# A hybrid decoder block on one core: GpSimd's low parts among mixing's last products wait for norm 2's last scaled half

## The chip, the cores and the metric

The kernel runs on one core of one Trainium2 chip. The time is the device time of one execution in microseconds. It was run three times before the change: 783.74, 784.01 and 784.80 us, median 784.01 us.

## The reference

One block of a decoder over 512 tokens of width 1024, all in float32:

```
h = rmsnorm(x, norm1_g);  z = h @ w_in + b_in          # 1024 -> 6656, five parts
u = glu(z);  u = conv31(u);  y_a = silu(layernorm(u)) @ conv_w_out + conv_b_out
xb = conv4(z_rx);  hb = rg_lru(xb);  y_b = (hb * gelu(z_rg)) @ lru_w_out
m = sigmoid(z_ga) * y_a + sigmoid(z_gb) * y_b
x = x + m @ w_mix_out
h = rmsnorm(x, norm2_g)
x = x + (silu(h @ ffn_w1) * (h @ ffn_w3)) @ ffn_w2      # 1024 -> 2816 -> 1024
out = rmsnorm(x, norm_f_g)
```

`rmsnorm(x, g)` is x / sqrt(mean(x * x) + 1e-6) * g over a row. What the change concerns lies between `x + m @ w_mix_out` and the first products of `h @ ffn_w1`.

## The kernel before

Every matrix product is made of three. A weight comes from HBM as a raw tile of 128x1024 in float32; ScalarE casts it to float32r (the high part, line 129), and VectorE or GpSimd subtracts the high part from the raw tile (the low part, line 125). TensorE then adds high by high, high by low and low by high. A chunk of weights is cast and split some chunks before it is used: `weights(key, ahead)` emits the chunks up to `ahead` behind the one that is asked for, so the casts and low parts of FFN weights are issued among mixing's last products. Which engine makes a low part is set where the chunk is listed. Of the first FFN chunks, `fb11_1`, `fb21_1` and `fb11_2` have GpSimd (`pool_e`), and `fb21_2` has VectorE. The buffers `hl_...` hold the two parts, `raw_...` the raw tile; eight raw tiles are in turn, and SyncE loads a new one once the low part made from the old one is done.

The larger products use seven products of half size in place of eight (Strassen's scheme), so their results are combined on VectorE from banks of PSUM. In `mix_end` (line 1478), mixing's last part, this is the order that is written out by hand for TensorE, ScalarE and VectorE:

- `second()`: the last products but those of the quarter `t4`; VectorE adds and subtracts the banks into `x2`, the residual stream in rows (four tiles of 128 tokens, `x2[t]`, in two halves of 512 columns each).
- For the first rows, t = 0 and 1: the root of the mean square (ScalarE, lines 686, 693 and 694; VectorE, lines 679 and 696), and then `scale` (line 1484): VectorE multiplies each half by it into `xs[t][half]`. Halves 0 of both rows come first, then halves 1; the last of the four is `xs11`. `newest["scaled"]` names the newest of these instructions.
- `newest["behind"]` is set to that last one while `third(i, range(2))` issues the products of `t4` for k = 0 and 1, and reset to None behind them. `third` asks for weights, so the cast and the low part of FFN chunks are emitted in this stretch.
- Twice: `turn_half` and two more products of `t4`. `turn_half` has TensorE transpose eight blocks of `xs` (line 712, banks `th`, four chunks of 128 columns by two rows). ScalarE copies each chunk out, multiplied by the norm's weight, as the high part `h20h` to `h27h` (line 715), and VectorE makes the low part `h20l` to `h27l` from the bank and the high part (line 716). Each of the second four chunks takes over the bank of one of the first four: `th04` waits for `h20l`, `th05` for `h21l`, and so on.
- Then GpSimd adds `h2` back from its parts (`full`, line 1476), VectorE finishes the other two rows, and these are scaled too.

Behind `mix_end` the FFN's first products begin: `b0.half` multiplies `h20` to `h27` of the first rows with `fb11_1` and `fb21_1` (banks `fr`, line 1584), `b1.half` with `fb11_2` and `fb21_2`; the second half of the rows is turned among them.

GpSimd's own order is not written out by hand: it takes its instructions as the scheduler places them, each with the waits that its data need. `tc.issue_after(i)` (line 133) orders the instructions of its block behind `i` only on the engine of `i` itself. As `newest["behind"]` is an instruction of VectorE, the line orders low parts on VectorE and says nothing on those of GpSimd.

Of the kernel before, what the change touches and what calls it, by code (L numbers as in the profile page):

```python
# [8 lines left out]
F32 = mybir.dt.float32  # L9
# [78 lines left out]
def tile_block(ctx, tc, a, out):  # L88
# [30 lines left out]
    newest = {}  # L119
    put_off = []  # L120

    SYNC = mybir.DependencyInfo(mybir.DependencyClass.Sync, mybir.DependencyReason.DATA)

    def sub(eng, o, x, y):
        return eng.tensor_tensor(out=o, in0=x, in1=y, op=ALU.subtract)  # L125

    def split_to(h, l, full, eng, copy=act.copy):

        newest["cast"] = copy(h, full)  # L129
        if eng is None:  # L130
            put_off.append((l, full, h.bitcast(F32)))
            return h, l
        with tc.issue_after(newest["behind"]) if newest.get("behind") else nullcontext():
            last = sub(eng, l, full, h.bitcast(F32))
        newest["sub" if eng is pool_e else "low"] = last.ins
        return h, l

# [16 lines left out]
    def split(name, full, eng, p_=None, copy=act.copy):  # L154
        p_ = p_ or pairt(name)
        return split_to(*p_, full, eng, copy)
# [25 lines left out]
    def emit_chunk():  # L182
        key, src, kt, cols, where, lo, after = chunks[emitted[0]]
        if emitted[0] not in loaded_raw:
            load_chunk(emitted[0])
        raw = loaded_raw.pop(emitted[0])
        emitted[0] += 1
        n = kt * cols
        rv = raw[:, :n]
        if where == "gate":  # L190
            hl = hls.tile([P, 2, 1024], F32R, tag="hl", name=f"hl_{key}")
            h = hl[:, 0, :n]
            after(rv, h)
            held[key] = h
        elif where == "hl" or callable(where):
            hl = hls.tile([P, 2, 1024], F32R, tag="hl", name=f"hl_{key}")

            if emitted[0] == 1:
                h, l = first_parts(hl[:, 0, :n], hl[:, 1, :n], rv)
            else:  # L200
                h, l = split_to(hl[:, 0, :n], hl[:, 1, :n], rv, lo, act.copy if emitted[0] > 2 else copy_halves)
            held[key] = (h.rearrange("p (k n) -> p k n", k=kt), l.rearrange("p (k n) -> p k n", k=kt))
            if after:
                after()
        else:
            held[key] = [
                split_to(longt(f"{key}h{i}", F32R), longt(f"{key}l{i}", F32R), rv[:, i * T : (i + 1) * T], lo)
                for i in range(2)
            ]
# [1403 lines left out]
    class Seven:  # L1613
# [14 lines left out]
        def copy(self):  # L1628
            self.c11 = shortt(f"c11_{self.k}")
            left_over(act.copy(self.c11, self.r1).ins)  # L1630
# [248 lines left out]
```

## Time and profile before

| What | Time (us) |
|---|---|
| three runs | 783.74, 784.01, 784.80; median 784.01 |
| profiled execution | 783.79 |
| its span, from the first instruction to the last | 782.0 |
| mean granted TensorE clock | 0.999 |
| norm 2's first scaling (line 1484) begins | 438.8 |
| the first FFN products begin (line 1584) | 446.2 |
| output products begin (line 1331, banks `or`) | 671.4 |

In the views of the profile a row of a timeline gives the start and the duration in us from the span's start, the engine, the line, the operation, the tiles (written from read, buffer numbers left out), the shapes, the count where rows were merged, and in brackets the idle time ahead and what ended it. PE is TensorE's matmuls, PEld its loads of the stationary operand, DVE VectorE, ACT ScalarE, POOL GpSimd, SPq the queue of SyncE. In a row of waits stand who waited and for whom, the sum in us, how often, and the longest. A row of the chain has start, duration and what it was. A tile's row has the least, the median and the longest duration in ns, and the first and last start.

### The profile page before, as it was taken

Reading aid. Unit: us, or ns where it says so; the run is one execution under the profiler, and the core shown is the slowest. Engines: PE = TensorE matmul, PEld = TensorE weight load, DVE = VectorE, ACT = ScalarE, POOL = GpSimd, SP = SyncE. Lnnn points to the kernel's source line nnn. Section 1 sums busy time; section 2 is a strip of 40 time slices with the busy share of each in tenths; the row PEclk is TensorE's granted clock in tenths of the full one; section 3 lists DMA queues with packets and bytes.
Section 4 is the critical chain, followed back from the end, with each engine's and each line's share of the span. In section 5 each row is a group of like instructions: output and inputs, shape, how many; then the busy total and the mean of one; then the engine's idle time right before and its main releaser. Section 6 shows DMA issues by size and latency. Waiting matters only on the chain.

```text
span 782.0 us, 12628 instructions
## 1 busy us (share of the span) xinstructions
PE 774.8 (99%) x4469; PEld 684.1 (87%) x4469; DVE 677.2 (87%) x1034; ACT 490.4 (63%) x739; POOL 289.7 (37%) x239
## 2 busy tenths in 40 slices
PE   9999999999999999999999999999999999999997
PEld 8988888888888888888998898999999999888886
DVE  6389998889997987799999869779888889999957
ACT  8543678976786687567564676445555455666844
POOL 4365856577677973211100581312222220000001
PEclk9999999999999999999999999999999999999999
DMA  8827978696999995399986577998989794679522
GB/s 247 233 57 205 257 211 235 174 270 196 258 239 281 314 277 189 115 251 326 304 278 186 160 246 226 231 309 199 277 222 253 251 212 135 216 228 306 169 68 107
DMA packets 184752, 174.39 MB, mean 223 GB/s; under 512 B 14682, under 2 KB 145906, under 8 KB 184690
## 3 DMA queue, kind: packets, MB, share of 16 engines
q1 hardware_dynamic: 166034, 131.39, 57.1%
q0 software_dynamic: 18496, 41.95, 22.6%
q8 instruction: 35, 0.57, 0.3%
q14 instruction: 27, 0.22, 0.1%
q10 hardware_dynamic: 160, 0.27, 0.1%
HBM read 149.97 MB, written 50.33 MB: 256 GB/s over the span
## 4 chain that ended last, share of the span: by engine, by line
PE 97%; DVE 1%; DMA 1%; ACT 0%; issue 0%; SPq 0%; DVEq 0%
PE z L667 36%; PE fr L1584 25%; PE or L1331 13%; PE yb L667 7%; PE ya L1408 5%; PE mxr L1331 4%; PE f L667 3%; PE g L1155 2%; PE fr L1647 1%; DMA x<-in_x_dram 1%; DVE xs L1484 1%; PE tx L728 0%; PE th L712 0%; PE z L785 0%; DVE x L125 0%; DVE x L116 0%
## 5 line engine op out<-in xcount | busy, mean ns | idle before, releaser
L920 DVE SCALAR_TENSOR_TENSOR cv<-u,par,cv 128x507 f32<-128x507 f32 (+15 forms) x240 | 162.1, 732 | 4.2 <-ACT cv L916 3.4
L125 POOL TENSOR_TENSOR hl_in<-raw_in,hl_in 128x1024 fp32r<-128x1024 f32 (+1 forms) x52 | 124.7, 2417 | 66.6 <-ACT hl_in L129 61.6
L1584 PE MATMUL fr<-hs_0h,hl_ft 128*128 128x256 f32 x320 | 59.2, 283 | 0.0
L129 ACT CAST hl_in<-raw_in 128x1024 fp32r<-128x1024 f32 x50 | 51.5, 1048 | 1.1 <-DMA th<-tg 0.8
L1584 PEld LDWEIGHTS fr<-hs_0h,hl_ft 128*128 128x128 f32 x320 | 50.6, 192 | 0.0
L125 POOL TENSOR_TENSOR hl_ot<-raw_ot,hl_ot 128x1024 fp32r<-128x1024 f32 x1 | 2.4, 2411 | 121.3 <-ACT hl_ot L129 121.3
L508 POOL DMA_DIRECT2D ot<-in_ffn_w_dram x24 | 26.4, 1112 | 54.3 <-DVE hl_ft L125 33.3
L1584 PE MATMUL fr<-hs_0l,hl_ft 128*128 128x256 f32 x160 | 45.3, 283 | 0.0
L129 ACT CAST hl_fb<-raw_fb 128x1024 fp32r<-128x1024 f32 x30 | 31.3, 1047 | 21.5 <-PE fr L1584 10.9
L125 DVE TENSOR_TENSOR hl_fb<-raw_fb,hl_fb 128x1024 fp32r<-128x1024 f32 x27 | 33.3, 1234 | 10.4 <-ACT hl_fb L129 9.4
L667 PE MATMUL z<-h10h,hl_in 128*128 128x512 f32 (+1 forms) x108 | 41.1, 382 | 0.0
L667 PE MATMUL z<-h13h,hl_in 128*128 128x512 f32 (+1 forms) x108 | 40.8, 379 | 0.0
L667 PE MATMUL z<-h11h,hl_in 128*128 128x512 f32 (+1 forms) x108 | 40.8, 379 | 0.0
L667 PE MATMUL z<-h15h,hl_in 128*128 128x512 f32 (+1 forms) x108 | 40.8, 379 | 0.0
L667 PE MATMUL z<-h17h,hl_in 128*128 128x512 f32 (+1 forms) x108 | 40.8, 379 | 0.0
L667 PE MATMUL z<-h12h,hl_in 128*128 128x512 f32 (+1 forms) x108 | 40.8, 379 | 0.0
L667 PE MATMUL z<-h16h,hl_in 128*128 128x512 f32 (+1 forms) x108 | 40.8, 379 | 0.0
L667 PE MATMUL z<-h14h,hl_in 128*128 128x512 f32 (+1 forms) x108 | 40.8, 379 | 0.0
L129 ACT CAST hl_ft<-raw_fb 128x1024 fp32r<-128x1024 f32 x28 | 28.6, 1049 | 14.9 <-DVE raw_fb L116 11.8
L117 POOL TENSOR_TENSOR fws<-fws 128x256 f32<-128x256 f32 x44 | 36.5, 830 | 2.1
L129 ACT CAST hl_ob<-raw_ob 128x1024 fp32r<-128x1024 f32 (+1 forms) x23 | 23.4, 1015 | 21.1 <-PE or L1331 14.7
L125 DVE TENSOR_TENSOR hl_ft<-raw_fb,hl_ft 128x1024 fp32r<-128x1024 f32 x28 | 33.6, 1217 | 1.2 <-ACT hl_ft L129 1.2
(965 smaller groups left out, 2682.8 us busy)
## 6 DMA issues: line engine op xcount, KB each, us to landing
raw_in<-in_w_in_dram SPq DMA_DIRECT2D x51, 512.0 KB
raw_fb<-in_ffn_w_dram SPq DMA_DIRECT2D x74, 256.0 KB
ot<-in_ffn_w_dram POOLq DMA_DIRECT2D x30, 512.0 KB, 8.1
raw_ob<-in_ffn_w_dram SPq DMA_DIRECT2D x33, 256.0 KB
raw_ot<-ot SPq DMA_DIRECT2D x33, 256.0 KB
fws<-in_ffn_w_dram SPq DMA_DIRECT2D x12, 512.0 KB
cot<-in_conv_w_out_dram POOLq DMA_DIRECT2D x12, 512.0 KB, 8.6
mxt<-in_w_mix_out_dram POOLq DMA_DIRECT2D x12, 512.0 KB, 9.6
```

The costliest lines, as they stand in the source:

```text
L117: plus_on = lambda eng, o, x, y: eng.tensor_tensor(out=o, in0=x, in1=y, op=ALU.add)
L125: return eng.tensor_tensor(out=o, in0=x, in1=y, op=ALU.subtract)
L129: newest["cast"] = copy(h, full)
L508: plus = lambda o, x: pool_e.dma_start(o, x, accum_op=ALU.add)
L667: pe.matmul(ps, l, r, start=i == 0, stop=i == n - 1)
L920: vec.scalar_tensor_tensor(out=acc[:, s:], in0=u[c][:, : T - s], scalar=dw(c, s), in1=acc[:, s:], op0=ALU.mult, op1=ALU.add)
L1155: pe.matmul(ps[:HB], head_chunk[0][:ROWS_G, g, h % 2, m, :], ext[h][m][:ROWS_G], start=m == 0, stop=m == 1)
L1331: pe.matmul(banks[i][:, cs], l_[:, ts], r_[:, cs], start=start and n == 0, stop=stop and n == 2, skip_group_check=again)
L1408: pe.matmul(ps[:, HALVES[i]], lw[:, c, cols], rx_, start=not (again or i or c or m), stop=bool(i and c == 3 and m == 2), skip_group_check= ...
L1484: newest["scaled"] = vec.tensor_scalar(out=sc[t][i], in0=x2[t][i], scalar1=r, scalar2=None, op0=ALU.mult).ins
L1584: pe.matmul(ps[:, HALVES[i]], lw[:, c, :], rx_, start=not (again or i or c or m), stop=bool(i and c == 3 and m == 2), skip_group_check=True,)
L1647: pe.matmul(self.r4[:, HALVES[i]], lw, rx_, start=not (i or c or m), stop=bool(i and c == 3 and m == 2), skip_group_check=True)
```

## The change

`split_to` no longer puts the subtraction into an `issue_after` block. The subtraction is issued as it is, and where `newest["behind"]` is set, the instruction gets a dependency of the class Sync on it: a wait on a semaphore when the two are on different engines.

```diff
@@ -130,8 +130,9 @@
         if eng is None:
             put_off.append((l, full, h.bitcast(F32)))
             return h, l
-        with tc.issue_after(newest["behind"]) if newest.get("behind") else nullcontext():
-            last = sub(eng, l, full, h.bitcast(F32))
+        last = sub(eng, l, full, h.bitcast(F32))
+        if newest.get("behind"):
+            tc.add_manual_dep(last.ins, newest["behind"].name, SYNC, reason="bank readers beside it")
         newest["sub" if eng is pool_e else "low"] = last.ins
         return h, l
 
```

The order of the instructions is the same on all engines. What differs is what GpSimd waits for at one place, among mixing's last products. Before, with the semaphores that each instruction waits for (one for each engine and DMA queue):

```order
L125 TENSOR_TENSOR hl_fb11_1_4452<-raw_fb11_1_4449,hl_fb11_1_4452 128x1024 [waits DMAHW1_49,DMAHW0_49,Activation_49]
L125 TENSOR_TENSOR hl_fb21_1_4510<-raw_fb21_1_4507,hl_fb21_1_4510 128x1024 [waits DMAHW2_49,DMAHW3_49,Activation_49,Pool_49]
L125 TENSOR_TENSOR hl_fb11_2_4548<-raw_fb11_2_4545,hl_fb11_2_4548 128x1024 [waits DMAHW4_49,DVE_49,DMAHW5_49,PE_49,Activation_49]
L1476 TENSOR_TENSOR hf0_4583<-h20h_4226,h20l_4227 128x256 [waits DVE_49]
L1476 TENSOR_TENSOR hf1_4585<-h21h_4228,h21l_4229 128x256 [waits DVE_49]
```

The same place of GpSimd's order with the change (behind line 132 all lines of the file are one further on):

```order
L125 TENSOR_TENSOR hl_fb11_1_4452<-raw_fb11_1_4449,hl_fb11_1_4452 128x1024 [waits DMAHW1_49,DMAHW0_49,Activation_49]
L125 TENSOR_TENSOR hl_fb21_1_4510<-raw_fb21_1_4507,hl_fb21_1_4510 128x1024 [waits DMAHW2_49,DVE_49,DMAHW3_49,Activation_49,Pool_49]
L125 TENSOR_TENSOR hl_fb11_2_4548<-raw_fb11_2_4545,hl_fb11_2_4548 128x1024 [waits DMAHW4_49,DMAHW5_49,PE_49,Activation_49]
L1477 TENSOR_TENSOR hf0_4583<-h20h_4226,h20l_4227 128x256 [waits DVE_49]
L1477 TENSOR_TENSOR hf1_4585<-h21h_4228,h21l_4229 128x256 [waits DVE_49]
```

The low part of `fb21_1` now also waits for VectorE's semaphore (DVE_49), for `xs11`. That of `fb11_2` waited for an earlier VectorE instruction, the reader of its buffer's former content; behind the new wait this one is always met and is left out.

On VectorE, this is where the instruction stands that is now waited for, `xs11`; VectorE's rows are those of before:

```order
L696 RECIPROCAL stats_139<-stats_139 128x1 [waits Activation_49]
L1484 TENSOR_SCALAR xs10_4457<-x210_3996,stats_139 128x512 [waits DVE_49]
L1484 TENSOR_SCALAR xs01_4456<-x201_3995,stats_139 128x512
L1484 TENSOR_SCALAR xs11_4458<-x211_3997,stats_139 128x512
L716 SCALAR_TENSOR_TENSOR h20l_4227<-th00_4525,par_101,h20h_4226 128x256 [waits Activation_49]
L716 SCALAR_TENSOR_TENSOR h21l_4229<-th01_4530,par_101,h21h_4228 128x256 [waits Activation_49]
```

Nothing moved here: `h20l` still follows `xs11` directly, and waits for ScalarE's copy `h20h`.

## The prediction

> **What bounds the kernel now.** I read the page first, then the chain of work that ended last in order of time, then the waits of TensorE.
>
> ```profile
> span 782.0 us, 12628 instructions
> PE 774.8 (99%) x4469; PEld 684.1 (87%) x4469; DVE 677.2 (87%) x1034; ACT 490.4 (63%) x739; POOL 289.7 (37%) x239
> PE 97%; DVE 1%; DMA 1%; ACT 0%; issue 0%; SPq 0%; DVEq 0%
> ```
>
> TensorE is busy 774.8 of 782.0 us, and 97% of the chain is its own work. An edit counts only where it moves TensorE. The chain leaves TensorE in one place in the middle of the span:
>
> ```profile
> 405.21 29.28 PE mxr L1331 x129
> ...
> 439.40 3.47 DVE xs L1484 x3
> 442.87 0.41 DVE h20l L716
> ...
> 443.32 1.61 PE th L712 x8
> 444.93 1.39 PE mxr L1331 x6
> 446.33 10.08 PE fr L1584 x84
> ```
>
> These are mixing's last products (`mxr`), norm 2's scaled halves of x (`xs`), the transposes of them (`th`) and the first FFN products (`fr`). Through 443.3 us the chain runs over VectorE, and 3.47 us of it are three scalings in a row. What TensorE loses there is in the waits: first those of its matmuls over the whole span, then those of its weight loads from 437 us on.
>
> ```profile
> PE warm L636 <- DVE ones L628: 1.1, 1, 1.1
> PE th L712 <- DVE h20l L716: 0.5, 1, 0.5
> PE tx L728 <- DVE x L768: 0.3, 1, 0.3
> ```
>
> ```profile
> PEld th L712 <- DVE h20l L716: 0.9, 1, 0.9
> PEld th L712 <- DVE h21l L716: 0.2, 1, 0.2
> PEld th L712 <- DVE h22l L716: 0.2, 1, 0.2
> PEld th L712 <- DVE h23l L716: 0.2, 1, 0.2
> ```
>
> The other two waits of matmuls lie at the program's start. So from 437 us to the end TensorE waits only for `h20l` to `h23l`, the low parts of the first four turned chunks, and that is the place of the change.
>
> **Why those low parts are late.** VectorE's timeline, with the tile's own row first (least, median and longest duration in ns):
>
> ```profile
> L1484 DVE TENSOR_SCALAR xs<-x,stats x8: 480/486/2669, 438.8 to 454.4; 128x512 f32<-128x512 f32 x8
> ```
>
> ```profile
> 439.40 3.47 DVE L1484 TENSOR_SCALAR xs<-x,stats 128x512 f32<-128x512 f32 x3
> 442.79 0.47 DVE L716 SCALAR_TENSOR_TENSOR h20l<-th,par,h20h 128x256 fp32r<-128x256 f32 x1
> 443.19 0.47 DVE L716 SCALAR_TENSOR_TENSOR h21l<-th,par,h21h 128x256 fp32r<-128x256 f32 x1
> ...
> 454.01 0.88 DVE L1484 TENSOR_SCALAR xs<-x,stats 128x512 f32<-128x512 f32 x2
> ```
>
> Two scalings in a row take 0.88 us, so one follows another by 0.88 - 0.48 = 0.40 us. The third of the first row thus began at 439.40 + 0.80 = 440.20 and lasted to 442.87: 2.67 us, the 2669 ns of the tile's row, against 0.48. It is `xs11`, the half on which the change makes GpSimd wait. GpSimd's timeline:
>
> ```profile
> 440.20 2.38 POOL L125 TENSOR_TENSOR hl_fb<-raw_fb,hl_fb 128x1024 fp32r<-128x1024 f32 x1 [4.18 <-ACT hl_fb L129]
> 443.44 2.38 POOL L125 TENSOR_TENSOR hl_fb<-raw_fb,hl_fb 128x1024 fp32r<-128x1024 f32 x1 [0.85 <-ACT hl_fb L129]
> ```
>
> The low part of `hl_fb21_1` runs from 440.20 to 442.58, and the scaling ends 0.29 us behind it. The same pair stands at the start of the program, VectorE's row first:
>
> ```profile
> 7.84 0.88 DVE L768 TENSOR_SCALAR x<-x,stats 128x512 f32<-128x512 f32 x1
> ```
>
> ```profile
> 7.83 0.61 POOL L140 CAST hl_in<-raw_in 128x512 fp32r<-128x512 f32 x1 [6.17 <-DMA raw_in<-in_w_in_dram]
> ```
>
> A scaling of 128x512 again meets a GpSimd instruction that began 0.01 us ahead of it, takes 0.88 us, and ends 0.28 us behind GpSimd's (8.72 against 8.44). Two stalls of 2.19 and 0.40 us, both released by GpSimd's end: I take the scaling to be shut out while GpSimd works. [...]
>
> **The change part by part.** No instruction is added or moved on any engine; the rows of the order are the same. One wait is added, on VectorE's semaphore, ahead of the low part of `hl_fb21_1`; the next low part, `hl_fb11_2`, loses a VectorE wait that has become needless.
>
> *xs11.* Without GpSimd beside it, it takes 0.48 us: 440.20 to 440.68, 2.19 us sooner.
>
> *GpSimd's low part.* It starts behind 440.68. GpSimd's start trails its releaser by 0.08 to 0.13 us: ScalarE's casts in the rows below end at 440.07 and 443.36, GpSimd starts at 440.20 and 443.44. So it runs from about 440.8 to 443.2. Behind it in GpSimd's queue stands `hl_fb11_2` at 443.44, which waits for the cast that ends at 443.36: it is not delayed. TensorE first reads the low part of `hl_fb21_1` in the third matmul of its group, at
>
> ```profile
> 449.28 0.28 PE L1584 MATMUL fr<-h24h,hl_fb 128*128 128x256 f32 x1
> ```
>
> that is 448.1 after the gain below, 4.9 us behind 443.2. The wait costs TensorE nothing. On SyncE's queue one load waits for this low part to give its raw buffer back:
>
> ```profile
> 442.61 0.38 SPq L179 DMA_DIRECT2D raw_f<-in_ffn_w_dram  x1
> ```
>
> It goes out 0.6 us later; the queue's next load follows `hl_fb11_2` and stays.
>
> *h20l to h23l.* ScalarE's rows:
>
> ```profile
> 439.04 1.03 ACT L129 CAST hl_fb<-raw_fb 128x1024 fp32r<-128x1024 f32 x1
> 440.86 0.47 ACT L715 ACTIVATE h20h<-th,par 128x256 fp32r<-128x256 f32 x1 [0.79 <-PE th L712]
> ...
> 441.94 0.48 ACT L715 ACTIVATE h23h<-th,par 128x256 fp32r<-128x256 f32 x1
> 442.30 1.06 ACT L129 CAST hl_fb<-raw_fb 128x1024 fp32r<-128x1024 f32 x1
> 443.80 0.47 ACT L715 ACTIVATE h24h<-th,par 128x256 fp32r<-128x256 f32 x1 [0.43 <-PE th L712]
> ```
>
> `h20l` needs `h20h`, ready at 441.33, so it starts at about 441.37 and not at 442.79. The others follow in steps of 0.40 (442.79 to 443.19 above), with `h23h` ready at 442.42: `h23l` starts at 442.57 and ends at 443.04.
>
> *TensorE.*
>
> ```profile
> 440.21 0.39 PE L1331 MATMUL mxr<-hl_mxt,mxvb1l 128*128 128x512 f32 x1
> 440.44 1.03 PE L712 MATMUL th<-ident,xs 128*128 128x128 f32 x8
> 441.23 0.71 PE L1331 MATMUL mxr<-hl_mxt,mxvb2h 128*128 128x512 f32 x2
> ...
> 442.46 0.39 PE L1331 MATMUL mxr<-hl_mxt,mxvb2l 128*128 128x512 f32 x1
> ```
>
> ```profile
> 443.32 1.61 PE L712 MATMUL th<-ident,xs 128*128 128x128 f32 x8 [0.47 <-DVE h20l L716]
> 444.69 0.48 PE L1331 MATMUL mxr<-hl_mxt,mxvb3h 128*128 128x512 f32 x1
> ```
>
> The first eight transposes began 0.23 us behind the product ahead of them (440.21 to 440.44) and handed over after 0.79 us (441.23). The second eight could have begun at 442.46 + 0.23 = 442.69, but began at 443.32: 0.63 us lost. They handed over after 1.37 us, since each pair waited for the next low part: 0.58 us lost. With `h20l` ready at 441.84 and `h23l` at 443.04, against 442.69 and about 443.28 (six transposes of 0.1 us later) at which TensorE wants their banks, both losses go: **0.63 + 0.58 = 1.21 us**. Bounds: 0.47 us if only the matmul row's idle time goes; 1.5 us, the sum of the four weight-load waits, from above. I take 1.21, since it compares two equal groups of eight.
>
> *What is late next.* The first FFN products want the bank that `h24l` frees, at 446.33 - 1.21 = 445.1. ScalarE can make `h24h` from 443.36 on, when its cast ends; `h24l` is then done at about 443.36 + 0.47 + 0.04 + 0.47 = 444.3. The second half's transposes start at
>
> ```profile
> 456.24 0.27 PE L712 MATMUL th<-ident,xs 128*128 128x128 f32 x1
> ```
>
> so they move to 455.03; their last scaled half is ready at 454.01 + 0.88 = 454.89 even if VectorE gained nothing. Past there no wait of TensorE is in the list, so it keeps the lead to the end.
>
> *The sum.* The profiled execution took 783.79 us: a span of 782.0 and 1.79 around it. 783.79 - 1.21 = 782.58. The median of the three runs before, 784.01, is 0.22 above that execution; on that footing it is 782.8.
>
> **The rivals.**
>
> *Part of the gain comes back.* The two margins above are thin: 0.24 us at the pair of `h23l`, 0.14 at 455.03. If `h20l` to `h23l` still paced the second eight, only 0.63 us would go: 783.2. Against it: VectorE has nothing else to do from 440.68 on, and will itself reach the later scalings sooner.
>
> *Nothing changes.* Something else held `xs11`, say the transfers around it. Then `xs11` still ends at 442.87, GpSimd's low part follows to 445.3, the next to 447.8, and TensorE, which reads them from 449.28 on, is neither helped nor hurt: 783.8. For it: two coincidences are few. [...] Against it: the load on SyncE's queue that needs that low part's end went out at 442.61, 0.03 us behind it, so the end is real.
>
> *Slower.* The low part is moved beside `h20l` to `h23l`. If GpSimd shut these out as it did the scaling, `h20l` would end at 443.2 + 0.29 = 443.49 (now 443.26), and `h21l` would meet the next low part and end at 445.82 + 0.29 = 446.11 (now 443.66): 2.45 us more, 786.2. It decides as soon as an operation with one input in PSUM can be shut out. Against it: `h22l` to `h27l` ran beside GpSimd's second low part (443.44 to 445.82) already, and the whole group is even:
>
> ```profile
> L716 DVE SCALAR_TENSOR_TENSOR h24l<-th,par,h24h x2: 470/476/483, 444.4 to 457.2; 128x256 fp32r<-128x256 f32 x2
> ```
>
> One of its two ran beside GpSimd, the other not: 470 and 483 ns.
>
> **How the numbers follow.** The whole 1.21 us: 0.72, 782.6. A part: 0.13, 783.2. Nothing: 0.11, 783.8. Slower: 0.04, 786.2. The runs before spread from 783.74 to 784.80, so I allow some 0.3 us of scatter around a median. The range of 781.9 to 783.6 covers the bound of 1.5 us (782.3) with scatter, and the part; it leaves out the last two cases. About what a measurement of this kernel can tell from no change is 0.2%, 1.57 us: faster means below 782.44 and slower above 785.58. The forecast lies 0.16 us short of that line; of its 0.72 I give 0.28 to the far side. Faster 0.28, same 0.68, slower 0.04.
>
> **What would show it.** Right: all eight `xs` rows at 0.48 us; GpSimd's low part at about 440.8, right behind `xs11`; the second eight transposes at 442.7 with no wait for `h20l`, and 0.8 us to the next product; the first `fr` product 1.2 us earlier, and the same lead at the end. Wrong: `xs11` still long (something else holds it); `h20l` to `h23l` over 0.47 us; or a wait of TensorE behind 446 us that is not in today's list.

## The result and the profile after

| | before | after |
|---|---|---|
| median of 22 runs each (us) | 783.97 (783.63 to 786.28) | 782.87 (782.40 to 784.05) |
| ratio of after to before | | 0.9986, 95% interval 0.9979 to 0.9992 |
| profiled execution (us) | 783.79 | 784.05 |
| first eight transposes (`th`) begin | 440.44 | 441.91 |

The kernel became 1.10 us faster by the medians, 0.6 to 1.6 us by the interval. The profiled execution of after, 784.05 us, is the longest of its 22, and its place of change lies 1.47 us later in the span. That offset comes from the start of the program, as shown at the end of this section, so below every time at the place is also given as a distance from the start of the first eight transposes, which I call T0.

The head of the page of after, with the span and the busy times of the engines:

```profile
span 782.2 us, 12628 instructions
PE 773.7 (99%) x4469; PEld 683.6 (87%) x4469; DVE 675.2 (86%) x1034; ACT 490.3 (63%) x739; POOL 289.8 (37%) x239
```

VectorE is busy 2.0 us less, which is roughly the length of the stall that the prediction spoke of, and GpSimd is busy as long as before. Next the chain of work of after at the place of the change:

```profile
406.68 35.40 PE mxr L1332 x156
442.08 0.88 PE th L713 x8
442.95 1.38 PE mxr L1332 x6
444.33 0.88 PE th L713 x8
445.21 1.37 PE mxr L1332 x6
446.58 10.07 PE fr L1585 x84
```

VectorE's pieces (`xs`, 3.47 us, and `h20l`) are out of the chain: it stays on TensorE from the products of mixing into the FFN. TensorE's waits over the whole span agree with that:

```profile
PE z L786 <- ACT h10h L738: 1.1, 1, 1.1
PE warm L637 <- DVE ones L629: 1.1, 1, 1.1
PE tx L729 <- DVE x L769: 0.9, 1, 0.9
```

All three lie at the program's start. Of the weight loads' waits from 437 us on, none is left, where before there were four. What VectorE and GpSimd do there now, VectorE's timeline first, with the row of the tile `xs` ahead of it in a fence of its own:

```profile
L1485 DVE TENSOR_SCALAR xs<-x,stats x8: 481/488/749, 440.3 to 455.5; 128x512 f32<-128x512 f32 x8
```

```profile
440.87 1.28 DVE L1485 TENSOR_SCALAR xs<-x,stats 128x512 f32<-128x512 f32 x3
442.84 0.48 DVE L717 SCALAR_TENSOR_TENSOR h20l<-th,par,h20h 128x256 fp32r<-128x256 f32 x1 [0.69 <-ACT h20h L716]
...
444.03 0.48 DVE L717 SCALAR_TENSOR_TENSOR h23l<-th,par,h23h 128x256 fp32r<-128x256 f32 x1
```

```profile
442.37 2.40 POOL L125 TENSOR_TENSOR hl_fb<-raw_fb,hl_fb 128x1024 fp32r<-128x1024 f32 x1 [4.88 <-ACT hl_fb L129]
```

The three scalings now take 1.28 us together (3.47 before), so the third, `xs11`, runs from 441.67 to 442.15. GpSimd's low part begins at 442.37, 0.22 us behind it. (Its row still names ScalarE's cast as what ended the idle time; but that cast had ended at 441.55, and where GpSimd waited for a cast alone it began 0.08 to 0.13 us behind it.) VectorE then waits 0.69 us for ScalarE before `h20l`: its lateness is gone, with time to spare. TensorE's timeline over the same stretch:

```profile
441.91 1.04 PE L713 MATMUL th<-ident,xs 128*128 128x128 f32 x8
442.71 0.71 PE L1332 MATMUL mxr<-hl_mxt,mxvb2h 128*128 128x512 f32 x2
...
443.93 0.40 PE L1332 MATMUL mxr<-hl_mxt,mxvb2l 128*128 128x512 f32 x1
444.17 1.04 PE L713 MATMUL th<-ident,xs 128*128 128x128 f32 x8
444.96 0.71 PE L1332 MATMUL mxr<-hl_mxt,mxvb3h 128*128 128x512 f32 x2
...
446.41 0.28 PE L1585 MATMUL fr<-h20h,hl_fb 128*128 128x256 f32 x1
```

The second eight transposes begin 0.24 us behind the product ahead and hand over after 0.79 us, just like the first eight. The distance from T0 to the second eight is 2.26 us (2.88 before); the first FFN products begin at T0 + 4.50 (5.72 before, from 440.44 to 446.16). So TensorE gained 1.22 us there, and its last matmul begins 1.22 us nearer to T0 as well (T0 + 334.65, before T0 + 335.87): nothing of the gain is given back later. This distance hardly scatters: e1 and e10 below, which keep the stall, have 335.85 to 335.87, and e2, e7 and e8, which do not, 334.65 to 334.66.

**Why the profiled execution of after is not shorter.** In ScalarE's timeline of after the first cast of a weight waits for its load:

```profile
8.70 0.62 ACT L140 CAST hl_in<-raw_in 128x512 fp32r<-128x512 f32 x1 [1.23 <-DMA raw_in<-in_w_in_dram]
```

In the execution of before this cast began at 7.60 without a wait:

```profile
7.60 0.60 ACT L139 CAST hl_in<-raw_in 128x512 fp32r<-128x512 f32 x1
```

TensorE waits 1.1 us for what follows (the row `z L786` above), and has the whole lag of 1.4 to 1.5 us by 12 us of the span. It keeps it until the place of the change, where it gets 1.22 back. When the first weights land thus moved one of these two executions by about as much as the effect in question; that it makes the scatter of the other runs too is not shown.

### The profile page after: what moved, and what is told of

It reads as the page before. It is cut to its first block, busy times and chain, and to the rows that moved or that the text cites. A ratio compares the mean times of both kernels' runs of the same rounds, so it can differ in the third digit from the quotient of the medians.

```text
span 782.2 us, 12628 instructions
## 1 busy us (share of the span) xinstructions
PE 773.7 (99%) x4469; PEld 683.6 (87%) x4469; DVE 675.2 (86%) x1034; ACT 490.3 (63%) x739; POOL 289.8 (37%) x239
## 4 chain that ended last, share of the span: by engine, by line
PE 98%; issue 1%; POOL 0%; ACT 0%; DVE 0%; POOLq 0%
PE z L668 36%; PE fr L1585 25%; PE or L1332 13%; PE yb L668 7%; PE ya L1409 5%; PE mxr L1332 5%; PE f L668 3%; PE g L1156 2%; PE fr L1648 1%; PE th L713 0%; PE z L786 0%; PE tx L729 0%; POOL hl_in L125 0%; ACT of L1822 0%; PE orl L1332 0%
```

## The experiments

**Theory A**, the prediction's: while a GpSimd instruction runs, a VectorE scaling from SBUF to SBUF beside it stands still (`xs11` 2.67 us in before, against 0.48), and the change removes the one place where that cost TensorE time. Why it stands still is in no trace; "the path" in the expectation of e9 is only a name for the cause. **The rivals**: something else held `xs11` (the transfers around it, the place in the order), or the low part can be put later still at no cost, or not at all without one.

| run | time, us | before beside it | ratio, 95% interval | `xs11`, us | GpSimd's low part, us | first `fr` behind T0, us |
|---|---|---|---|---|---|---|
| before | 783.97 | | | 2.67 | 2.38 | 5.72 |
| after | 782.87 | 783.97 | 0.9986 (0.9979 to 0.9992) | 0.48 | 2.40 | 4.50 |
| e1 | 783.89 | 783.68 | 1.0005 (0.9996 to 1.0014) | 2.67 | 2.38 | 5.72 |
| e2 | 782.68 | 783.68 | 0.9986 (0.9978 to 0.9995) | 0.48 | 2.43 | 4.51 |
| e3 | 783.12 | 783.68 | 0.9992 (0.9984 to 1.0001) | 1.56 | 1.28 and 1.48 | 4.60 |
| e4 | 782.82 | 783.68 | 0.9989 (0.9980 to 0.9998) | 0.48 | none beside it | 4.67 |
| e5 | 787.57 | 783.59 | 1.0047 (1.0032 to 1.0062) | 0.48 | 2.4 | 4.51 |
| e6 | 791.26 | 783.59 | 1.0096 (1.0079 to 1.0113) | 0.48 | 2.34 | 4.50 |
| e7 | 782.50 | 783.59 | 0.9986 (0.9976 to 0.9995) | 0.74 | 2.40 | 4.50 |
| e8 | 782.41 | 783.59 | 0.9985 (0.9976 to 0.9994) | 0.68 | 2.93 | 4.50 |
| e9 | 783.98, one run | 784.21, one run | | 2.16 | 2.38 | 5.99 |
| e10 | 783.64, one run | 784.21, one run | | 1.89 | 2.38 | 5.72 |
| e11 (e5 again) | 786.27, one run | 784.21, one run | | 0.48 | 2.4 | 4.51 |

The last three columns are read from each run's own profile; they tell far more than the times, whose scatter is as large as the effect. (e3's interval reaches 1.0001, so its time alone shows no gain.)

### e1: the wait on a scaling that is already done

```diff
             rs = [scaled(t, 1, (0,)) for t in range(2)]
+            on = newest["scaled"]
             for t in range(2):
                 scale(t, 1, rs[t])
 
-            newest["behind"] = newest["scaled"]
+            newest["behind"] = on
```

> The changed kernel, but GpSimd's low part waits for xs10, the second of the four scaled halves, in place of xs11. xs10 is done before ScalarE's cast, so the wait is met and GpSimd starts where it did without it. Theory A (VectorE's scaling is shut out while a GpSimd instruction that began ahead of it runs): xs11 takes 2.7 us again, and from the first eight transposes to the first fr product it is 5.7 us as before (4.5 with the change); time as before, 784.0. Theory B (the wait as such, or the instruction it adds, is what helps): 4.5 us and 782.9.

Measured, VectorE's timeline and then GpSimd's:

```profile
439.20 3.46 DVE L1485 TENSOR_SCALAR xs<-x,stats 128x512 f32<-128x512 f32 x3
```

```profile
440.00 2.38 POOL L125 TENSOR_TENSOR hl_fb<-raw_fb,hl_fb 128x1024 fp32r<-128x1024 f32 x1 [4.18 <-ACT hl_fb L129]
```

All is as before, with the third scaling again at 2.67 us. A wait as such, or the changed code of `split_to`, does nothing. What counts is that the low part is pushed behind `xs11`.

### e2: the wait on the scaling ahead of xs11

```diff
-            for t in range(2):
-                scale(t, 1, rs[t])
+            scale(0, 1, rs[0])
+            on = newest["scaled"]
+            scale(1, 1, rs[1])
 
-            newest["behind"] = newest["scaled"]
+            newest["behind"] = on
```

> The changed kernel, but GpSimd's low part waits for xs01, the third scaled half. It then starts about 0.1 us behind xs01, when VectorE has begun xs11 already. Theory A, with whoever starts first keeping the other out: xs11 takes 0.48 us, the low part is the one that is held, by up to 0.3 us (2.4 to 2.7 us long); 4.5 us from the first transposes to the first fr product, 782.9. Theory A without the first-come part (GpSimd always wins): xs11 2.5 us, 5.6 us, 783.9. Theory C (something else than GpSimd holds xs11, say the transfers): no tie to where GpSimd starts, 5.7 us, 784.0.

```profile
440.01 1.28 DVE L1485 TENSOR_SCALAR xs<-x,stats 128x512 f32<-128x512 f32 x3
```

```profile
441.11 2.43 POOL L125 TENSOR_TENSOR hl_fb<-raw_fb,hl_fb 128x1024 fp32r<-128x1024 f32 x1 [4.49 <-ACT hl_fb L129]
```

GpSimd began at 441.11, while `xs11` (440.81 to 441.29) was running, and the scaling took its usual 0.48 us. So a wait on `xs01` does as well: it was enough here that VectorE's instruction began first, by 0.30 us. GpSimd's 2.43 us are only 0.03 above its usual time, though 0.18 us overlapped. The test of who waits is weak here, since the overlap is short; e8 and the end of e9 and e10 come back to it.

### e3: the low part in two halves

```diff
-            last = sub(eng, l, full, h.bitcast(F32))
+            if newest.get("behind") and eng is pool_e:
+                for cs in (slice(0, T), slice(T, 2 * T)):
+                    last = sub(eng, l[:, cs], full[:, cs], h[:, cs].bitcast(F32))
+            else:
+                last = sub(eng, l, full, h.bitcast(F32))
```

This is made from the kernel before, with no wait added.

> The kernel before, without the wait; GpSimd makes the low part of hl_fb21_1 in two instructions of 512 columns, the first at the same moment. Theory A, held for one instruction: the first half lasts 1.2 to 1.3 us, xs11 ends 0.3 us behind it and takes 1.3 to 1.5 us, h20l starts at once, and 4.6 to 4.7 us pass from the first transposes to the first fr product; 783.0. If GpSimd keeps VectorE out over both instructions: xs11 2.7 us, 5.7 us, 784.0. Theory C: xs11's length has nothing to do with GpSimd's, 2.7 us, 784.0.

```profile
439.01 2.36 DVE L1488 TENSOR_SCALAR xs<-x,stats 128x512 f32<-128x512 f32 x3
```

```profile
439.81 1.28 POOL L125 TENSOR_TENSOR hl_fb<-raw_fb,hl_fb 128x512 fp32r<-128x512 f32 x1 [4.18 <-issue]
```

`xs11` ran from 439.81 to 441.37: it was held for the first half of GpSimd's work (to 441.09) and ended 0.28 us behind it, not behind the second. Here the hold lasted as long as one instruction of GpSimd, and the scaling took 1.56 us where 1.3 to 1.5 were expected. This half of the stall already gives 1.12 of the 1.22 us, since TensorE did not need `h20l` before T0 + 2.25.

### e4: the low part on VectorE

```diff
-                f_both(n, k, vec if (n, k) == ("b21", 2) else pool_e)
+                f_both(n, k, vec if n == "b21" else pool_e)
```

> The kernel before, without the wait; VectorE makes the low part of hl_fb21_1, behind xs11 and ahead of h20l, in 1.22 us. Theory A: with GpSimd idle xs11 takes 0.48 us, the low part ends 1.2 us behind it, h20l starts 0.5 us later than with the change and h23l is 0.3 us late for its transposes: 4.7 to 4.9 us from the first transposes to the first fr product, 783.2. Theory C: xs11 2.7 us and the low part behind it, 7 us, 785.2.

With GpSimd idle there, the three scalings took 1.28 us without any wait:

```profile
439.23 1.28 DVE L1484 TENSOR_SCALAR xs<-x,stats 128x512 f32<-128x512 f32 x3
440.42 1.22 DVE L125 TENSOR_TENSOR hl_fb<-raw_fb,hl_fb 128x1024 fp32r<-128x1024 f32 x1
441.55 0.48 DVE L716 SCALAR_TENSOR_TENSOR h20l<-th,par,h20h 128x256 fp32r<-128x256 f32 x1
```

So the hold of before (2.67 us) went with GpSimd's instruction. The low part costs VectorE 1.22 us here, which is mostly hidden: the first `fr` is 0.17 us later than with the change.

### e5 and e11: the low part still later

```diff
-                turn_half("th", xs, "norm2_g", h2p, 0, [bank, bank2], range(4 * q, 4 * q + 4))
+                turned_ = turn_half("th", xs, "norm2_g", h2p, 0, [bank, bank2], range(4 * q, 4 * q + 4))
+                if q == 0:
+                    tc.add_manual_dep(newest["held"][0], turned_[1].name, SYNC, reason="later")
```

Made from the kernel after, whose own wait is left out; `newest["held"]` lists the GpSimd low parts of this stretch.

> The changed kernel, but the low part of hl_fb21_1 waits for h23l, 2.3 us behind xs11. It then runs from 2.6 to 5.0 us behind the first transposes' start, and that of hl_fb11_2 behind it to 7.4. The prediction put the lead of the first at 4.9 us, so TensorE should still not wait: 4.5 us from the first transposes to the first fr product, no wait of TensorE behind it, 782.9. If the lead was over-estimated by more than half: a wait of an fr product for GpSimd, and some us more.

The expectation failed: 787.57 us, slower than before. At the place itself all went as with the change (first `fr` at T0 + 4.51). The loss is in the second half of the rows. GpSimd's and VectorE's timelines:

```profile
442.87 4.77 POOL L125 TENSOR_TENSOR hl_fb<-raw_fb,hl_fb 128x1024 fp32r<-128x1024 f32 x2 [7.14 <-DVE h23l L717]
...
454.53 0.90 POOL L508 DMA_DIRECT2D ot<-in_ffn_w_dram  x1
455.47 2.35 POOL L125 TENSOR_TENSOR hl_ft<-raw_ft,hl_ft 128x1024 fp32r<-128x1024 f32 x1
```

```profile
452.04 1.94 DVE L1485 TENSOR_SCALAR xs<-x,stats 128x512 f32<-128x512 f32 x2
...
454.09 4.03 DVE L1485 TENSOR_SCALAR xs<-x,stats 128x512 f32<-128x512 f32 x2
```

```profile
PE th L713 <- DVE xs L1485: 3.2, 1, 3.2
```

The tile's row of e5:

```profile
L1485 DVE TENSOR_SCALAR xs<-x,stats x8: 481/632/3328, 438.5 to 454.8; 128x512 f32<-128x512 f32 x8
```

The two low parts end at 447.64, or T0 + 7.49, where after has T0 + 5.41. GpSimd's whole queue is 2.1 us later: the last of its sums `hf` run beside the first two scalings of the other rows (1.94 us for the two), and its next low part, `hl_ft`, the last two (4.03 us, ending 458.12, again 0.30 us behind GpSimd's end at 457.82). TensorE waits 3.2 us for these. The last scaling alone took 3.33 us, from 454.79 on. It began 0.68 us ahead of `hl_ft`, while GpSimd's DMA issue was still running (to 455.43), and was let through neither there nor before `hl_ft` had ended: here a hold went over from one instruction of GpSimd to the next, which began 0.04 us behind it. In after the same low part waits for a cast and begins at T0 + 14.59, behind the last scaling (455.07 + 0.88 = 455.95, T0 + 14.04).

The profiled execution took 785.66 us, the three others 787.42 to 788.41 at a mean granted clock of 0.997 to 0.995 against 0.998. e11 ran the same kernel once more, to see whether the clock falls behind the wait:

> Question: the kernel of e5 once more, for a second profile. In e5 the profiled execution took 785.66 us at a mean granted clock of 0.998, the three others 787.42 to 788.41 at 0.997 to 0.995; in e6 TensorE ran at a granted clock of 0.50 for 5.6 us behind its wait of 6.5 us. Theory A (TensorE's wait of 3.2 us for the second rows' scaling sometimes brings the clock down to a half behind it): a time of 787.4 to 788.4 comes with a stretch of some 4 to 6 us at 0.50 right behind 458 us, and loses half of it; a time of about 785.7 comes with none. Rival B (something else is late in the slower executions): a time of 787 or more with a clock of 1.00 from 455 to 466 us, and a further wait of TensorE in the list.

It took 786.27 us, with the same wait of 3.2 us, a granted clock of 1.00 throughout the stretch, and T0 0.61 us later than in e5, which is all of its difference to 785.66. So none of the longer executions was profiled. Theory A of e11 is neither shown nor excluded, and what costs the longer ones their further 2 us is open; what e6 shows of the clock, below, makes it plausible.

### e6: the low part 11 us later than in after

```diff
-                plus(2 + i, 0, r7[i])
+                done_ = plus(2 + i, 0, r7[i])
+            tc.add_manual_dep(newest["held"][0], done_.ins.name, SYNC, reason="later")
```

Made from the kernel after in the same way as e5.

> The changed kernel, but the low part of hl_fb21_1 waits for VectorE's last sum from the banks r7; GpSimd's order then has it behind the eight sums hf. By the timelines it ends 13 to 14 us behind the first transposes' start, and TensorE wants it 7.6 us behind it: here the lead is used up and the wait moves to an fr product (one wait of 5.5 to 6.5 us), 788.3 to 789.5. If the lead were bound by something else than this low part: no such wait, 782.9.

The wait came as expected, the time did not:

```profile
PE fr L1586 <- POOL hl_fb L125: 6.5, 1, 6.5
```

From T0 to its last matmul TensorE took 343.94 us in the profiled execution, 9.3 more than the 334.65 of after, and not 6.5 more. A table by stages (stretch, its length, TensorE's busy time and matmuls, granted clock, share of the DMA engines, GB/s) shows the rest:

```profile
446.00:448.50 2.50, 2.50 (x23) 1.00 0.33 83
448.50:455.00 6.50, 0.16 (x2) 0.67 0.38 129
455.00:460.80 5.80, 5.64 (x26) 0.50 0.69 221
460.80:466.00 5.20, 5.20 (x45) 0.99 1.02 329
```

Behind the wait, TensorE worked at half its clock for 5.6 us. The matmuls of 128x256 there follow one another by 0.21 us, where those ahead of the wait did by 0.12. From the last product ahead of the wait to the first behind it 6.78 us passed in place of 0.12, or 6.7 lost; the other 2.6 of the 9.3 us are the slow clock. In e6's trace the clock is 1.00 up to 450.7 us and 0.50 from there, 2.05 us behind the end of the last matmul at 448.66. (The table's 0.67 says the same: 2.2 us at 1.00 and 4.3 at 0.50 make 6.5.)

The slow stretch lasted 10.2 us, from 450.7 to 460.9 (the table's 0.99 says that 0.1 us of its last stretch was at 0.50). In e5 and e11, with a wait of 3.2 us, the clock was 1.00 from 455 to 466 us, over the wait and behind it. Whether a wait of that length ever costs the clock is not shown.

### e7 and e8: what xs11 reads

Both are made from the kernel before, where GpSimd's low part begins within 0.01 us of `xs11`. e7 gives `xs11` one input in a bank of PSUM:

```diff
-            for t in range(2):
-                scale(t, 1, rs[t])
+            scale(0, 1, rs[0])
+            newest["scaled"] = vec.scalar_tensor_tensor(out=sc[1][1], in0=x2[1][1], scalar=rs[1], in1=r7[0], op0=ALU.mult, op1=ALU.add).ins
```

> The kernel before, without the wait; xs11 is made with an operation that has one input in SBUF and one in PSUM (it adds the bank r7, so the values of one half of the rows are not the norm's). GpSimd starts at the same moment as before. [...] If VectorE is shut out whatever its operation: xs11 over 2.6 us, 5.7 us, 784.0.

e8 has two inputs in SBUF in place of one and a factor:

```diff
-            for t in range(2):
-                scale(t, 1, rs[t])
+            scale(0, 1, rs[0])
+            newest["scaled"] = vec.tensor_tensor(out=sc[1][1], in0=x2[1][1], in1=x2[1][0], op=ALU.mult).ins
```

> The kernel before, without the wait; xs11 is a product of two halves of x in SBUF (it leaves out the norm's factor). [...]

e7, VectorE and GpSimd:

```profile
440.20 0.74 DVE L1508 SCALAR_TENSOR_TENSOR xs<-x,stats,mxr 128x512 f32<-128x512 f32 x1
```

```profile
440.20 2.40 POOL L125 TENSOR_TENSOR hl_fb<-raw_fb,hl_fb 128x1024 fp32r<-128x1024 f32 x1 [4.19 <-ACT hl_fb L129]
```

Neither holds the other (0.74 and 2.40 us). e8, the same two rows:

```profile
439.89 0.68 DVE L1508 TENSOR_TENSOR xs<-x,x 128x512 f32<-128x512 f32 x1
```

```profile
439.89 2.93 POOL L125 TENSOR_TENSOR hl_fb<-raw_fb,hl_fb 128x1024 fp32r<-128x1024 f32 x1 [4.19 <-ACT hl_fb L129]
```

e7 rules out that VectorE is held whatever its operation (0.74 us, not over 2.6). But its operation differs from the scaling as well as its input, and these runs do not part the two. In e8 VectorE went through too, in 0.68 us, and GpSimd was 0.53 us longer. Either an instruction with two inputs in SBUF is let through, or the two began too close together to say which was first. e9 and e10 decide that.

### e9 and e10: in the middle of GpSimd's low part

Both put the instruction of e7, which was not held (0.74 us), ahead of `xs11`, so that it begins 0.78 us behind GpSimd's low part. e9 then has the product of e8:

```diff
-            for t in range(2):
-                scale(t, 1, rs[t])
+            scale(0, 1, rs[0])
+            vec.scalar_tensor_tensor(out=sc[1][1], in0=x2[1][1], scalar=rs[1], in1=r7[0], op0=ALU.mult, op1=ALU.add)
+            newest["scaled"] = vec.tensor_tensor(out=sc[1][1], in0=x2[1][1], in1=x2[1][0], op=ALU.mult).ins
```

> Question: the kernel before, but VectorE first runs an instruction with one input in a bank (0.74 us, not held in e7), and behind it xs11 as a product of two halves in SBUF. This puts the two-input instruction some 0.6 us behind the start of GpSimd's low part, where e8 had the two within 0.01 us. (The values of one half of the rows are not the norm's.) Theory A (whichever of the two begins first has the path until its end): the product begins at about +0.4 from the first eight transposes and ends 0.29 behind GpSimd's end, at +2.4 (2.0 us instead of 0.68); GpSimd's low part stays at 2.40; h20l at +2.35, the first fr at +5.7. Theory B (a product of two SBUF inputs is let through, and GpSimd pays): 0.68 us, GpSimd's low part 2.9, h20l at about +1.0, the first fr at +4.5 to +4.6.

e10 has the scaling as it was, `scale(1, 1, rs[1])`, in place of the last line.

> The counterpart of e9: the same instruction with a bank input ahead, and behind it xs11 as the scaling that it is in the kernel before. Both theories expect a scaling that comes in the middle of GpSimd's low part to be held: it begins at about +0.4, ends at +2.4 (2.0 us instead of 0.48), h20l at +2.35, the first fr at +5.7, the time of before (783.8). If it takes 0.5 us, only instructions that begin together with GpSimd's are held, and the reading of the whole place falls.

e9, VectorE and GpSimd:

```profile
440.11 0.74 DVE L1508 SCALAR_TENSOR_TENSOR xs<-x,stats,mxr 128x512 f32<-128x512 f32 x1
440.88 2.16 DVE L1509 TENSOR_TENSOR xs<-x,x 128x512 f32<-128x512 f32 x1
```

```profile
440.11 2.38 POOL L125 TENSOR_TENSOR hl_fb<-raw_fb,hl_fb 128x1024 fp32r<-128x1024 f32 x1 [4.11 <-ACT hl_fb L129]
```

e10, VectorE; GpSimd's low part ran from 440.06 to 442.44:

```profile
440.84 1.89 DVE L1484 TENSOR_SCALAR xs<-x,stats 128x512 f32<-128x512 f32 x1
```

Both kinds were held to GpSimd's end. The product ends 0.55 us behind it (443.04 against 442.49), the scaling 0.29 us. So neither was let through: in e8 the product had come first, and the 2.93 us are GpSimd's wait. The lengths bear that out. GpSimd's low part grew by 0.53 us in e8 where 0.68 overlapped, by 0.20 in e3's second half (1.48 against 1.28) where 0.33 overlapped, and by 0.03 in e2 where 0.18 did: each time by the overlap less 0.13 to 0.15. The first `fr` came at T0 + 5.99 in e9 and at 5.72 in e10, where 5.7 was expected for both.

## Why the prediction was right

*The cause.* Right. e4 (no GpSimd instruction there: `xs11` 0.48 us), e3 (half a one, half the hold: 1.56 us) and e7 (an operation with an input in a bank, no hold: 0.74 us) each remove the stall or part of it in another way, and the time from T0 to the first `fr` goes with it; e1 keeps the overlap and the stall (2.67 us). The rival "nothing changes", by which something else held `xs11`, falls with e4 and e7, whose loads and order up to it are those of before. Whether the one that starts first holds the other cannot be seen at 440.20, where the two starts lie within 0.01 us; e8 and e9 together show that order counts (the same product took 0.68 us where it began with GpSimd's low part, and 2.16 us where it began 0.77 us behind). The runs show who is held, by what and until when; the reason is in no trace.

*xs11 and GpSimd's low part.* Right: 0.48 us. GpSimd began 0.22 us behind it, where I had taken 0.08 to 0.13 from waits on ScalarE. Measured from T0, the low part ran from 0.46 to 2.86, and the next began at 3.00, as before. The step held with 0.14 us to spare.

*What the wait costs.* The sum had it at nothing, since TensorE reads this low part 4.9 us later. It did cost nothing (4.8 us measured: ready at 444.77, read at 449.53). But the reason was incomplete, as e5 shows: with the low part still ready ahead of its reader there, 3.2 us were lost to the queue behind it. What protected the change is the other half of the step, that the next low part waits for a cast anyway, and that margin is the 0.14 us. How far the queue could move beyond it, short of the 2.1 us of e5, before TensorE loses anything was not run.

*TensorE's gain.* 1.21 us forecast, as 0.63 and 0.58. Measured from T0: 2.88 - 2.26 = 0.62 ahead of the second eight, and 1.37 - 0.79 = 0.58 within them; 1.22 to the first `fr`.

*What is late next.* Nothing was. `h23l` was ready at 444.51, and its bank was wanted at 444.17 + 0.6 = 444.77: a margin of 0.26, forecast 0.24. The second half's transposes began at T0 + 14.58 and their last scaled half was ready at T0 + 14.04, a margin of 0.54. The forecast's 0.14 was the case in which VectorE gained nothing. This is the margin that e5 used up.

*Two signs failed as they stood.* "`h20l` to `h23l` over 0.47 us" was a sign of being wrong, and they took 0.48. That is no hold: with GpSimd idle `h20l` took 0.48 us as well (e4). And "all eight `xs` rows at 0.48 us" does not hold: one took 749 ns. It is in VectorE's row, beside GpSimd's:

```profile
453.82 1.15 DVE L1485 TENSOR_SCALAR xs<-x,stats 128x512 f32<-128x512 f32 x2
```

```profile
453.85 0.90 POOL L508 DMA_DIRECT2D ot<-in_ffn_w_dram  x1
```

GpSimd issues a DMA there, and no TensorE wait follows. In the profile of before the two did not meet.

*The rival that ended slower* (low parts shutting out `h20l` to `h23l`) fell, as in after `h20l` to `h23l` ran beside GpSimd's low part at 0.48 us each. The prediction's argument had a wrong reading in it: of the two `h24l` it took the one of 483 ns to have run without GpSimd, but GpSimd's `hl_ft` ran from 455.71 to 458.29, and that `h24l` began at 457.17. The row with GpSimd idle is e4's.

*The time.* 782.6 forecast on the profiled execution, 782.8 on the median's footing; 782.87 measured. The interval of the ratio ends at 0.9979 and 0.9992, on both sides of the line of 0.2%, so which side of it the true gain lies on stays open, and 1.22 us is 0.16%. For its chances the prediction put the forecast 0.16 us short of that line, but it took 782.6, on the profiled execution's footing, against a line drawn from the median; 782.8 is 0.36 short, so its chance of 0.28 for the far side rests on that slip.

No version of these beat the kernel after: e2, e7 and e8 reach the same first `fr`, within 0.01 us. Behind it TensorE has no wait left to take away before the end.

## What to carry to other kernels

Look in a tile's row for an instruction whose longest time is far above its median, and put the other engine's timeline beside it: a VectorE scaling that is too long and ends 0.3 us behind a GpSimd instruction was held by it here. With GpSimd idle ahead of it, it was enough to let VectorE's urgent one begin first (0.48 us in after and e2, against 2.67 in before); cutting GpSimd's into pieces (1.56 us, e3) and an operation with one input in PSUM (0.74 us, e7) helped too. In e5, where two of GpSimd's instructions were 0.04 us apart, a hold outlasted the one in which it began (3.33 us). When work is pushed back on a queue, count how far the instructions behind it move, and what they then meet; that the pushed one is still ready for its own reader says little.

## What the runs showed of the hardware

- Two VectorE forms were held by a GpSimd subtraction from SBUF to SBUF, the scaling by a factor (ends 0.28 to 0.30 us behind GpSimd, in before, e3, e5 and e10) and the product of two SBUF halves (0.55 us behind, e9); `scalar_tensor_tensor` with one input in a bank was not (0.74 us, e7). The product held GpSimd in e8 (2.93 us against 2.40) and was held in e9 (2.16 us against 0.68). The recorded starts did not always tell who was first: within 0.01 us GpSimd won in before and VectorE in e8, and in e5 and e6 a scaling that began 0.68 and 0.10 us ahead of GpSimd's `hl_ft`, during the DMA issue before it, was held to the end of `hl_ft`.
- A scaling beside a DMA issue of GpSimd's took 0.749 us instead of 0.48.
- After a wait of 6.5 us TensorE ran at a granted clock of 0.50 for 5.6 us, which added 2.6 us to the wait (e6); the clock had fallen 2.05 us into the wait. After 3.2 us it did not (1.00 from 455 to 466 us in e5 and e11, as profiled).
- The first weights landed later in after than in before: the first cast began at 8.70 us and not at 7.60, and TensorE was 1.4 to 1.5 us late by 12 us of the span, as much as this change is worth.
